# A decode and prefill layer on one core: where passes over cache pages are issued, and which engine takes two products

## The chip, the core and the metric

The kernel runs on one core of a Trainium2 chip. A core has five engines that work side by side, each with its own queue in order: TensorE (PE, matmuls into PSUM), VectorE (DVE), ScalarE (ACT), GpSimd (POOL) and SyncE (SP, which here only issues DMAs). The metric is the device time of one execution in microseconds (us); the median of several runs counts.

## What is computed

One layer of a hybrid decoder, for a prompt of 512 tokens with 16 meta tokens before it, and for eight single new tokens ("sequences"), each with 2048 past positions in a paged cache. An input projection of 2048 columns to 8192 feeds two groups of eight heads, whose gated outputs meet in one output projection:

```python
hq, hk, hv, log_f, hg, aq, ak, av, ag = project(h, norm_g, w_in, lb)   # one matmul, split in eight
S, o = hgrn2_chunked(hq, hk, hv, log_f, s0, chunk)                     # HGRN2 group: a gated linear recurrence
# differential attention group
s = einsum('bqhcd,bkhcd->bchqk', q, k) * 64 ** -0.5 + bias             # c = 0, 1: two softmaxes per head
p = softmax(s, axis=-1)
w = p[:, 0] - lam * p[:, 1]
o_at = einsum('bhqk,bkhv->bqhv', w, v)
h = h + concat(norm(o_hg) * silu(hg), norm(o_at) * silu(ag)) @ w_out   # then a final norm
k_past = cache_k[page_table]                                           # eight sequences x 16 pages of 128 tokens
v_past = cache_v[page_table]
```

For the eight sequences the attention runs over 128 pages of keys and 128 pages of values, 0.5 MB each (128 tokens by 8 heads by 128).

## The kernel before

**The projections set the pace.** The weights are taken in 80 blocks of 128 columns: 64 of the input projection (8 each of aq, ak, av, then hf, hi and hq in turn, then hg, then ag) and 16 of the output projection. A block has four groups of four 128-row pieces. `load_raw` brings weights, `split` (L322) makes a rounded high part on ScalarE (tile hi) and a rest on VectorE (tile lo), three groups ahead (LEAD), and `group` (L337) issues 24 matmuls into the tile ps. The main loop writes one group after another, and between two of them (one "slot") it steps what else is due: `step_threads` runs each waiting generator to its next yield, `value_step` may issue one step of values on TensorE, and `fill` adds VectorE passes over pages. So the order on every engine is fixed when the program is written, and each engine works in that order.

**The kernel's own clock.** While it is written, the program keeps an estimated time for each engine and tile (class `Clock`, L76). Every engine call goes through `Counted` (L141), which estimates its cost and moves that clock; for this reason nearly all instructions have the line L151 in the profile, and tiles tell them apart.

**Prompt attention.** After the block av of a head, `attn` (L910) makes four steps per head, one of 128 queries each, in a pipeline over slots. Scores go to a PSUM tile sc; VectorE adds the bias into the tiles p (two softmaxes) with a row minimum; ScalarE takes the exponential and the sum. Two steps later VectorE makes the reciprocals r, the second one times the factor lambda; ScalarE multiplies the second p by r (L973); then VectorE joins both into p (L976). A step on, TensorE transposes p (tile t_w), and a step after that multiplies values (tile o).

**Keys of the pages.** `page_step` (L675) works on VectorE in two halves per page: page times query (tiles pgt and qb), then a sum over each head's half (tile scd). It may start a sequence s only when the softmax weights of sequence s - 2 are there (flag w) and the values of sequence s - 3 are done (flag pv, KA = 3). Key pages have three buffers (NKB); each finished step issues the next page load on SP's queue. After 16 pages `softmax_dec` makes the weights (tile wd).

**Values of the pages.** For sequences 0 to 5, `value_step` (L702) multiplies two pages by their weights on TensorE: four matmuls of 32 columns side by side (eight records, tile t_pv), and VectorE adds the outcome into acc. Sequences 6 and 7 are named in ONV (L282): for them `dve_value_step` (L733) multiplies a page by the weights head by head on VectorE, eight instructions a page into a tile in the buffer qb, and `pv_sum` (L761) sums over partitions on TensorE at the end. It begins only when the keys of all sequences are done (L741), and each sequence waits for the one before.

**When passes are issued.** `fill` (L603) is called once in a slot and at a few other places. It adds passes as long as VectorE's estimated time is under TensorE's plus LATE (L601), which has a value for each of four stretches: before the block av0, until the last attention head, until the last HGRN head, and after. A key page not landed by then is skipped in favour of a page of values.

**The end of the input projection.** Before the second group of block 63 (L1326), a loop goes on until the norms of all heads and sequences have been written; pages that are left are issued there. The output projection begins after that block.

Of the kernel before, what the change touches and what calls it, by code (L numbers as in the profile page):

```python
# [75 lines left out]
class Clock:  # L76
# [28 lines left out]
                t = b  # L105
        return t

    def issue(self, e, cost, outs, ins, latency=0.08, shared=False):
        start = self.now[e]
        for table, aps in ((self.written, ins + outs), (self.read, outs)):  # L110
            for ap in aps:
                t, by = table.get(ap.tensor.name, (0.0, e))
                if by != e:
                    start = max(start, t + self.LATENCY)
        if e == "pool":
            start = self.port(start)
            self.pool_held = start + cost
        elif shared:
            start = max(start, self.pool_held)
            a, b = self.held[-1]  # L120
            self.held = self.held[-40:]
            if start - b < 0.03:
                self.held[-1] = (a, start + cost)
            else:
                self.held.append((start, start + cost))
        self.now[e] = end = start + cost
        end += latency
        for ap in ins:
            n = ap.tensor.name
            self.read[n] = max(self.read.get(n, (0.0, "")), (end, e))  # L130
        for ap in outs:
            self.written[ap.tensor.name] = end, e
# [6 lines left out]


class Counted:  # L141


    def __init__(self, eng, clock, name):
        self.eng, self.clock, self.name = eng, clock, name

    def __getattr__(self, op):
        f = getattr(self.eng, op)

        def call(*a, **k):  # L150
            r = f(*a, **k)  # L151
            aps = [x for x in a if hasattr(x, "free_size")]
            outs = [x for x in (k.get("out"), k.get("accum_out")) if x is not None]
            if "out" not in k:
                outs.append(aps.pop(0))
            ins = aps + [x for n, x in k.items() if hasattr(x, "free_size") and n not in ("out", "accum_out")]
            n = max(ins[0].free_size(), 1) if op == "tensor_reduce" else (outs[-1] if "out" not in k else outs[0]).free_size()
            late, shared = 0.08, False
            from_psum = any(in_psum(x) for x in ins + outs)
            wide = [x for x in ins if x.free_size() > 1 and not in_psum(x)]  # L160
            if self.name == "pe":
                late = 0.165
                if op == "transpose":
                    t = 0.11
                elif ap_dtype(ins[0]) == F32R:
                    t = max(0.11, n / 2400 + 0.0115)
                else:
                    t = 2 * max(0.118, n / 1200 + min(ins[0].free_size(), P) / 1200)
                    if ins[0].partition_size() == 64:
                        t /= 2  # L170
                    if ins[0].free_size() == 32:
                        t /= 4
            elif self.name == "dve":
                two = op in ("scalar_tensor_tensor", "tensor_tensor_reduce")
                one = op in ("tensor_scalar", "tensor_copy") and not from_psum
                t = (0.13 if two or op == "tensor_scalar" else 0.075) + n / (1920 if one else 960) * (2 if op == "tensor_tensor_scan" else 1)
                if op == "tensor_tensor_reduce":
                    t += 0.13
                shared = len(wide) >= 2 or one and n > 64
            elif self.name == "act":  # L180
                t = n / 1200 + (0.055 if from_psum else 0.095) + (0.09 if hasattr(k.get("scale"), "free_size") or k.get("accum_out") is not None else 0)
            else:
                t = 0.07 + n / 430
            self.clock.issue(self.name, t, outs, ins, late, shared)
            return r
        return call
# [11 lines left out]
def layer_kernel(ctx: ExitStack, tc: tile.TileContext, A):  # L198
# [80 lines left out]

    GK = 4  # L280
    NKB, NPB = 3, 2
    ONV = (6, 7)  # L282
    NG = KC // GK
    LEAD = 3

# [312 lines left out]
                threads.remove(th)  # L598
        return ran

    LATE, SOON = (3.0, 1.5, 4.0, 4.0), 0.0  # L601

    def fill():  # L603

        ph = 0 if "av0" not in flags else 1 if "attn7" not in flags else 2 if "hgrn7" not in flags else 3
        while clock["dve"] < clock["pe"] + LATE[ph]:
            if turn_v[0] and dve_value_step():
                turn_v[0] = 0
                continue
            i = done[0]  # L610
            if i < len(kloaded) and any(clock.written[t.tensor.name][0] > clock["pe"] + SOON for t in (kloaded[i], qbs[ksteps[i][0]])):
                if not dve_value_step():
                    break
                continue
            turn_v[0] = 1
            if not page_step() and not dve_value_step():
                break

    def later(slots, **k):

# [54 lines left out]
    def page_step():  # L675

        i = done[0]
        if i >= len(ksteps):
            return False
        s, g = ksteps[i]  # L680
        z = half[0]
        if z == 0:
            if flags.get("q", slot[0]) >= slot[0] or g == 0 and (s >= 2 and f"w{s - 2}" not in flags or s >= KA and f"pv{s - KA}" not in flags):
                return False
            load_keys(i + 1)
            if g == 0:
                scs[s] = sm.tile([P, NPG + 1, 2 * H], F32, name="scd", bufs=2)
        pt = kloaded[i]
        if z == 0:
            V.tensor_tensor(pt, pt, qbs[s], op=ALU.mult)  # L690
        else:
            V.tensor_reduce(scs[s][:, g, :], pt.rearrange("p (a d) -> p a d", d=64), axis=AX.X, op=ALU.add)
        half[0] = 1 - z
        if z:
            if g == NPG - 1:
                load_q(s + 1)
                spawn(softmax_dec(s), "snew", *([f"w{s - 1}"] if s else []))
            done[0] += 1
            load_keys(i + 1 + NKB)
        return True  # L700
# [32 lines left out]
    def dve_value_step(landed=True):  # L733

        n = vtaken[0]
        s, i = divmod(n, NPG)
        if n >= len(vloaded) or s not in ONV:
            return False
        if flags.get(f"w{s}", slot[0]) >= slot[0] or i == 0 and s and flags.get(f"pv{s - 1}", slot[0]) >= slot[0]:
            return False  # L740
        if i == 0 and done[0] < len(ksteps):  # L741
            return False
        pt = vloaded[n]
        if landed and clock.written[pt.tensor.name][0] > clock["dve"]:
            return False
        if i == 0:
            accs[s] = pg.tile([P, H * P], F32, name="qb", tag="qb")
        for h in range(H):
            cs, w = slice(h * P, (h + 1) * P), ws[s][:, i, h:h + 1]
            if i == 0:  # L750
                V.tensor_scalar(accs[s][:, cs], pt[:, cs], w, None, op0=ALU.mult)
            else:
                V.scalar_tensor_tensor(accs[s][:, cs], pt[:, cs], w, accs[s][:, cs], op0=ALU.mult, op1=ALU.add)
        vtaken[0] += 1
        vdone[0] = vtaken[0] // VB
        load_values()
        if i == NPG - 1:
            spawn(pv_sum(s))
        return True
# [67 lines left out]
    def decode_q():  # L827
        for b in range(2):
            qs = hw.tile([NS, 512], F32, name="qs", tag="t3", bufs=2)
            t = tp("t_q")  # L830
            for h in range(4):
                T.transpose(t[:NS, h * P:(h + 1) * P], aq[:, b * 4 + h, S0:S0 + NS], ident)
            S.activation(qs, t[:NS, :], AF.Copy, scale=-1.0)
            store(out=qd[:, b * 512:(b + 1) * 512], in_=qs)
        load_q(0)
        load_keys(NKB)
        load_values()
        flag("q")
        yield

    def decode_snew():
# [68 lines left out]
    def attn():  # L910
        live = {}
        for n in range(4 * H + 4):
# [53 lines left out]
            if i2:  # L966
                a, jj = i2["head"], i2["j"]
                L1 = (jj + 1) * P + NM
                p0, p1 = i2["p"]
                r = sm.tile([P, 2], F32, name="r")  # L970
                V.reciprocal(r, a["s1"][:, jj, :])
                V.tensor_scalar(r[:, 1:2], r[:, 1:2], nlam, None, op0=ALU.mult)
                S.activation(p1[:, :L1], p1[:, :L1], AF.Copy, scale=r[:, 1:2])  # L973
            fill()
            if i2:
                V.scalar_tensor_tensor(p0[:, :L1], p0[:, :L1], r[:, 0:1], p1[:, :L1], op0=ALU.mult, op1=ALU.add)  # L976
            if n < 4 * H:
                a = head
# [426 lines left out]
```

## Time and profile before

| | |
|---|---|
| median of 3 runs | 1261.57 us (1259.65 to 1262.13) |
| profiled execution | 1256.73 us, of which the span shown is 1254.9 us |
| TensorE busy | 1214.3 us (97%) |
| VectorE busy | 844.9 us (67%) |
| ScalarE busy | 547.8 us (44%) |
| GpSimd busy | 144.7 us (12%) |

A line of a profile names the source line, the engine, the operation, the tile written and the tiles read, and sizes as partitions by elements. Matmuls overlap one another, so a busy TensorE isn't TensorE at its peak. Stretches are given in us from the start of the span: queries and keys are projected until about 250, prompt attention runs until about 460, HGRN until about 900, the gates until 1046, the output projection until the end.

### The profile page before, as it was taken

The numbers are of one execution on the slowest core, as the hardware profiler recorded it, in microseconds if no ns is written. First come the engines' busy times: TensorE is split into PE (matmuls) and PEld (weight loads), VectorE is DVE, ScalarE is ACT, GpSimd is POOL, SyncE is SP. The second block draws the span as 40 slices with busy tenths as digits, with TensorE's granted clock in tenths as the row PEclk, the third lists the DMA queues.
The fourth block names the chain that finished last, engine by engine and source line by source line (L and its number), as shares of the span: only waits on it lengthen the run. The fifth ranks groups of instructions, "written<-read, shape, count | busy, mean of one in ns | idle before, by whom it ended". The sixth has DMA issues, their size and how long they took to land.

```text
span 1254.9 us, 24952 instructions
## 1 busy us (share of the span) xinstructions
PE 1214.3 (97%) x9412; PEld 1096.5 (87%) x9412; DVE 844.9 (67%) x1527; ACT 547.8 (44%) x1288; POOL 144.7 (12%) x151
## 2 busy tenths in 40 slices
PE   8999999999999999999998999999999999999995
PEld 6899999976777779888787888888999999999995
DVE  6522598865666578878668788888997936355253
ACT  6322323355555664545445455554432235223233
POOL 2000001100000001111012010122131410021020
PEclk9999999999999999999999999999999999999998
DMA  7353788935645576889796897987787636433223
GB/s 230 95 161 97 239 275 283 285 103 189 191 163 188 183 234 190 297 272 305 256 318 193 296 307 256 323 286 247 226 287 226 204 101 217 122 89 96 86 68 137
DMA packets 240956, 261.02 MB, mean 208 GB/s; under 512 B 8783, under 2 KB 198962, under 8 KB 240171
## 3 DMA queue, kind: packets, MB, share of 16 engines
q1 hardware_dynamic: 57298, 164.09, 37.5%
q10 hardware_dynamic: 183538, 95.34, 26.9%
q8 instruction: 74, 1.21, 0.4%
q14 instruction: 46, 0.38, 0.1%
HBM read 245.94 MB, written 16.14 MB: 209 GB/s over the span
## 4 chain that ended last, share of the span: by engine, by line
PE 86%; DVE 5%; DMA 4%; ACT 3%; issue 1%; ACTq 1%; SPq 0%; DVEq 0%
PE ps L151 69%; PE t_pv L151 4%; PE o L151 2%; PE ho L151 2%; PE sc L151 1%; DMA raw<-in_w_out 1%; DMA pgt<-in_cache_v 1%; DVE qb L151 1%; PE up L151 1%; PE t_w L151 1%; DVE lo L151 1%; PE at L151 1%; DVE scd L151 1%; PE t_ra L151 1%; PE t_y L151 1%
## 5 line engine op out<-in xcount | busy, mean ns | idle before, releaser
L151 PE MATMUL ps<-xh,hi 128*128 128x264 f32 (+2 forms) x2048 | 539.2, 294 | 3.9 <-ACT gate L151 2.2
L151 PE MATMUL ps<-xl,hi 128*128 128x264 f32 (+2 forms) x2048 | 521.8, 285 | 1.1 <-DVE xl L151 1.1
L151 PEld LDWEIGHTS ps<-xh,hi 128*128 128x128 f32 x2048 | 386.7, 189 | 58.2 <-issue 48.2
L151 PEld LDWEIGHTS ps<-xl,hi 128*128 128x128 f32 x2048 | 386.8, 189 | 2.6 <-issue 2.5
L151 DVE TENSOR_TENSOR lo<-raw,hi 128x512 fp32r<-128x512 f32 x321 | 244.1, 765 | 198.9 <-ACT hi L151 198.3
L151 PE MATMUL ps<-xh,lo 128*128 128x264 f32 (+2 forms) x2048 | 333.8, 285 | 0.0
L151 ACT CAST hi<-raw 128x512 fp32r<-128x512 f32 x321 | 196.3, 617 | 228.7 <-PE ps L151 187.5
L151 PEld LDWEIGHTS ps<-xh,lo 128*128 128x128 f32 x2048 | 284.6, 189 | 0.0
L151 DVE TENSOR_TENSOR pgt<-pgt,qb 128x1024 f32<-128x1024 f32 x128 | 163.7, 1279 | 14.5 <-DMA pgt<-in_cache_k 11.3
L151 DVE TENSOR_REDUCE scd<-pgt 128x16 f32<-128x1024 f32 x128 | 155.0, 1211 | 0.1
L151 PE MATMUL ps<-mh,hi 128*128 128x256 f32 (+1 forms) x512 | 130.0, 286 | 0.5 <-ACT y L151 0.5
L151 PE MATMUL ps<-ml,hi 128*128 128x256 f32 (+1 forms) x512 | 128.5, 283 | 0.0
L151 PEld LDWEIGHTS ps<-mh,hi 128*128 128x128 f32 x512 | 96.4, 188 | 1.0 <-ACT y L151 0.7
L151 PEld LDWEIGHTS ps<-ml,hi 128*128 128x128 f32 x512 | 96.5, 188 | 0.0
L151 PE MATMUL ps<-mh,lo 128*128 128x256 f32 (+1 forms) x512 | 82.5, 283 | 0.0
L151 DVE SCALAR_TENSOR_TENSOR qb<-pgt,wd,qb 128x128 f32<-128x128 f32 x240 | 70.9, 364 | 0.0
L151 PEld LDWEIGHTS ps<-mh,lo 128*128 128x128 f32 x512 | 70.3, 188 | 0.0
L151 PE MATMUL t_pv<-pgt,wd 128*32 128x512 f32 x384 | 53.9, 605 | 12.7 <-ACT wmT L151 4.2
L151 DVE SCALAR_TENSOR_TENSOR p<-p,r,p 128x144 f32<-128x144 f32 (+3 forms) x32 | 18.2, 568 | 71.3 <-ACT p L151 71.2
L151 DVE TENSOR_TENSOR acc<-acc,t_pv 128x512 f32<-128x512 f32 x42 | 28.7, 682 | 23.9 <-PE t_pv L151 23.9
L151 POOL TENSOR_TENSOR sd<-sd,vb 128x1024 f32<-128x1024 f32 x8 | 20.1, 2509 | 183.4 <-ACT vb L151 156.5
L151 ACT COPY hgm<-ho 128x128 f32<-128x128 f32 x32 | 8.5, 265 | 69.5 <-PE ho L151 59.6
(242 smaller groups left out, 1167.2 us busy)
## 6 DMA issues: line engine op xcount, KB each, us to landing
pgt<-in_cache_k SPq DMA_DIRECT2D x128, 512.0 KB
pgt<-in_cache_v SPq DMA_DIRECT2D x128, 512.0 KB
raw<-in_w_in ACTq DMA_DIRECT2D x125, 512.0 KB
raw<-in_w_out ACTq DMA_DIRECT2D x32, 512.0 KB
x<-in_x_prompt SPq DMA_DIRECT2D x4, 1024.0 KB
qb<-qd SPq DMA_DIRECT2D x8, 512.0 KB
sd<-in_state_hgrn SPq DMA_DIRECT2D x8, 512.0 KB
vb<-hvd SPq DMA_DIRECT2D x8, 512.0 KB
```

Of the source, the lines that this page charges most:

```text
L151: r = f(*a, **k)
```

## The change

Three things are changed together.

- **Passes wherever VectorE would wait.** `Counted` gets a hook, `meanwhile`. Before an instruction of VectorE is written, the kernel compares the time at which its inputs are ready by the clock (`ready`, taken out of `issue`) with VectorE's time. As long as the difference is over WAIT = 1.1 us, it writes one more pass: a half of a key page or a page of values (`page`, the choice that `fill` made before). The hook is set when the decode queries are ready. It is off within a pass and within `fill` (`aside`). In the hook a page counts as ready if it has landed 0.3 us after VectorE's time. LATE goes from (3.0, 1.5, 4.0, 4.0) to (2.0, 0.0, 0.5, 3.0).
- **The second softmax's factor.** The multiplication of the second p by r moves from ScalarE to VectorE, right before the instruction that joins both.
- **Three sequences' values on VectorE.** ONV goes from (6, 7) to (5, 6, 7).

```diff
-    def issue(self, e, cost, outs, ins, latency=0.08, shared=False):
-        start = self.now[e]
+    def ready(self, e, outs, ins):
+
+        start = 0.0
         for table, aps in ((self.written, ins + outs), (self.read, outs)):
             for ap in aps:
                 t, by = table.get(ap.tensor.name, (0.0, e))
                 if by != e:
                     start = max(start, t + self.LATENCY)
+        return start
+
+    def issue(self, e, cost, outs, ins, latency=0.08, shared=False):
+        start = max(self.now[e], self.ready(e, outs, ins))
...
 class Counted:
+    WAIT = 1.1
...
+            if self.meanwhile:
+                step, self.meanwhile = self.meanwhile, None
+                while self.clock.ready(self.name, outs, ins) - self.clock[self.name] > self.WAIT and step():
+                    pass
+                self.meanwhile = step
+            r = f(*a, **k)
...
-    ONV = (6, 7)
+    ONV = (5, 6, 7)
...
-    LATE, SOON = (3.0, 1.5, 4.0, 4.0), 0.0
+    LATE, SOON = (2.0, 0.0, 0.5, 3.0), 0.0
+
+    def page(at):
+
+        if turn_v[0] and dve_value_step():
+            turn_v[0] = 0
+            return True
+        i = done[0]
+        if i < len(kloaded) and any(clock.written[t.tensor.name][0] > at for t in (kloaded[i], qbs[ksteps[i][0]])):
+            return dve_value_step()
+        turn_v[0] = 1
+        return page_step() or dve_value_step()
 
     def fill():
 
         ph = 0 if "av0" not in flags else 1 if "attn7" not in flags else 2 if "hgrn7" not in flags else 3
...
+        while clock["dve"] < clock["pe"] + LATE[ph] and aside(lambda: page(clock["pe"] + SOON)):
+            pass
+
+    def aside(step):
+
+        keep, V.meanwhile = V.meanwhile, None
+        r = step()
+        V.meanwhile = keep
+        return r
...
         flag("q")
+        V.meanwhile = lambda: page(clock["dve"] + 0.3)
         yield
...
-                S.activation(p1[:, :L1], p1[:, :L1], AF.Copy, scale=r[:, 1:2])
             fill()
             if i2:
+                V.tensor_scalar(p1[:, :L1], p1[:, :L1], r[:, 1:2], None, op0=ALU.mult)
                 V.scalar_tensor_tensor(p0[:, :L1], p0[:, :L1], r[:, 0:1], p1[:, :L1], op0=ALU.mult, op1=ALU.add)
```

## Rows read from the trace of the kernel before

**Rows 1.** The page: span, busy time of each engine, chain that ended last.
```profile
span 1254.9 us, 24952 instructions
PE 1214.3 (97%) x9412; PEld 1096.5 (87%) x9412; DVE 844.9 (67%) x1527; ACT 547.8 (44%) x1288; POOL 144.7 (12%) x151
...
PE 86%; DVE 5%; DMA 4%; ACT 3%; issue 1%; ACTq 1%; SPq 0%; DVEq 0%
```
**Rows 2.** Waits of TensorE: who waited for whom, us total, times, longest.
```profile
PE t_pv L151 <- ACT wmT L151: 4.2, 6, 0.7
...
PE t_pv L151 <- DVE wd L151: 3.7, 1, 3.7
PE t_pv L151 <- DVE st L151: 2.6, 3, 1.0
PE ps L151 <- ACT gate L151: 2.2, 3, 0.9
...
PE t_pv L151 <- DVE scd L151: 0.6, 1, 0.6
```
**Rows 3.** Busy time by stretches: length, each engine (instructions), TensorE's clock, DMA.
```profile
300.00:325.00 25.00, 23.95 (x161) 18.40 (x160) 15.87 (x45) 13.59 (x42) 0.71 (x4) 1.00 0.52 174
...
675.00:700.00 25.00, 21.33 (x156) 18.65 (x155) 19.20 (x25) 9.48 (x26) 5.21 (x4) 0.93 0.77 244
...
900.00:925.00 25.00, 24.12 (x198) 23.71 (x198) 24.92 (x80) 8.10 (x16) 7.13 (x5) 1.00 0.91 295
...
1025.00:1050.00 25.00, 25.00 (x210) 25.00 (x209) 15.84 (x33) 14.13 (x28) 2.35 (x3) 1.00 0.30 86
```
**Rows 4.** TensorE in order of time: start, duration, instruction, idle time before it.
```profile
287.02 1.06 PE L151 MATMUL t_pv<-pgt,wd 128*32 128x512 f32 x8 [0.71 <-ACT wmT L151]
288.01 0.39 PE L151 MATMUL ps<-xh,hi 128*128 128x272 f32 x1
...
952.17 1.05 PE L151 MATMUL t_pv<-qb,ones 128*32 128x512 f32 x4
953.15 0.39 PE L151 MATMUL ps<-xh,hi 128*128 128x256 f32 x1
```
**Rows 5.** Groups of VectorE by shape: count, busy us, mean ns, idle before.
```profile
L151 DVE SCALAR_TENSOR_TENSOR qb<-pgt,wd,qb 128x128 f32<-128x128 f32 x240 | 70.9, 364 | 0.0
L151 DVE TENSOR_TENSOR acc<-acc,t_pv 128x512 f32<-128x512 f32 x42 | 28.7, 682 | 23.9 <-PE t_pv L151 23.9
...
L151 DVE TENSOR_SCALAR qb<-pgt,wd 128x128 f32<-128x128 f32 x16 | 4.4, 350 | 0.0
...
L151 DVE TENSOR_SCALAR xr<-xr,rfin 128x512 f32<-128x512 f32 x6 | 2.6, 483 | 1.3 <-ACT rfin L151 1.3
```
**Rows 6.** The tile pgt: ns min/median/max, first and last start us, shapes.
```profile
L151 DVE SCALAR_TENSOR_TENSOR qb<-pgt,wd,qb x240: 329/340/1386, 902.7 to 1004.5; 128x128 f32<-128x128 f32 x120
...
L151 DVE TENSOR_TENSOR pgt<-pgt,qb x128: 1203/1216/2522, 139.6 to 896.5; 128x1024 f32<-128x1024 f32 x128
L151 DVE TENSOR_REDUCE scd<-pgt x128: 1187/1211/1220, 141.3 to 898.8; 128x16 f32<-128x1024 f32 x128
```
**Rows 7.** Groups of ScalarE by shape, the factor on the second p.
```profile
L151 ACT ACTIVATE p<-p,r 128x528 f32<-128x528 f32 x8 | 5.8, 720 | 0.0
...
L151 ACT ACTIVATE p<-p,r 128x144 f32<-128x144 f32 x8 | 3.2, 400 | 0.0
```
**Rows 8.** Waits of VectorE: us total, times, longest.
```profile
DVE p L151 <- ACT p L151: 71.2, 30, 5.5
```
**Rows 9.** VectorE's busy time with the tile scd, by stretches.
```profile
225.00:250.00 25.00, 8.79 (x10) 1.00 0.90 284
...
400.00:425.00 25.00, 2.42 (x2) 1.00 0.59 191
```
**Rows 10.** The tile mh: matmuls of the output projection, first and last start.
```profile
L151 PE MATMUL ps<-mh,hi x512: 274/283/391, 1045.9 to 1240.3; 128*128 128x256 f32 x86, 128*128 128x264 f32 x85
```
**Rows 11.** VectorE in order of time: the last norm of the sequences' attention.
```profile
1018.89 0.28 DVE L151 SCALAR_TENSOR_TENSOR oSa<-oSa,gat,sqs 128x64 f32<-128x64 f32 x1
```

More of the change, by code (lines that the diff above doesn't have):

```diff
@@ L141 @@
 class Counted:
+    WAIT = 1.1
     def __init__(self, eng, clock, name):
         self.eng, self.clock, self.name = eng, clock, name
+        self.meanwhile = None
     def __getattr__(self, op):
@@ L150, in call @@
         def call(*a, **k):
-            r = f(*a, **k)
             aps = [x for x in a if hasattr(x, "free_size")]
@@ L599, in step_threads @@
         return ran
-    LATE, SOON = (3.0, 1.5, 4.0, 4.0), 0.0
+    LATE, SOON = (2.0, 0.0, 0.5, 3.0), 0.0
[8 more added lines that the diff above has]
+        return page_step() or dve_value_step()
     def fill():
         ph = 0 if "av0" not in flags else 1 if "attn7" not in flags else 2 if "hgrn7" not in flags else 3
[L606 to L617, printed above, removed]
+        while clock["dve"] < clock["pe"] + LATE[ph] and aside(lambda: page(clock["pe"] + SOON)):
[5 more added lines that the diff above has]
+        return r
     def later(slots, **k):
```

## The prediction

> **What bounds the kernel now.** I read the page's busy shares first, then the chain of work that ended last, then the waits of TensorE, and only then the other engines. The reader is to see in the first two that TensorE is the bound: it is busy 97% of the span, and 86% of the chain runs through it [rows 1]. The waits of TensorE say how little of this is waiting: the longest kinds are 4.2, 3.7, 2.6 and 2.2 us [rows 2]. So a cut in VectorE's or ScalarE's work is worth nothing by itself; what counts is work taken from TensorE, and the few us for which it stands still. VectorE has room, but unevenly: 15.9 us of 25 busy in the attention stretch, 19.2 in the HGRN stretch, 24.9 in the stretch that multiplies values [rows 3]. The last is where a VectorE bound could come from.
>
> **Part 1, sequence 5's values go from TensorE to VectorE (ONV).** On TensorE a value step is eight matmul records; one starts at 287.02 and the next projection matmul at 288.01, so it holds the array for 0.99 us [rows 4]. A sequence has eight steps: 7.9 us leave. The new sum over partitions (pv_sum) comes in once; its like ran from 952.17 to 953.15, 0.98 us [rows 4]. The transposes at the end are as many as before. Net: 6.9 us less on TensorE, which is on the path. I count no further wait with it, since a wait before a value step may pass to whatever stands there next; if it goes too, that belongs to the larger gain below.
> On VectorE, seven additions of 0.68 us and one copy, bounded by the same row, go: 5.5 us. In come 8 products at 0.350 and 120 at 0.364 us [rows 5]: 46.5 us, so 41 us more. They cost nothing as long as they end before TensorE needs them; that cover is worked out under the rivals, as it is the weak point.
> Here two rows speak for caution: one product of this kind took 1386 ns against a median of 340, and one page multiply 2522 against 1216 [rows 6]. If one product in each of the 48 pages were held as the longest was, 48 x 1.05 = 50 us would be added to VectorE; by the mean of the row, which has in it what this trace had of such holds, nothing is. I take the mean and carry the 50 us into the last rival. The Trainium skill, page "SBUF — State Buffer", section "Who interferes with whom", gives holds a cause: a VectorE instruction with two SBUF inputs and a GpSimd instruction that reads SBUF exclude each other for a whole instruction. By that rule the end would be the slower rival's; by the row's mean it is the forecast's.
>
> **Part 2, the second softmax's factor goes from ScalarE to VectorE.** ScalarE loses 32 activations, 5.8 us for the eight widest and 3.2 for the eight narrowest, so about 18 us in all over four widths [rows 7]. VectorE gains 32 one-source multiplies by a column. The nearest rows are 350 ns at 128 elements and 483 at 512 [rows 5]; the widths here are 144 to 528, so 11 to 16 us; I take 13.5. What goes is VectorE's wait for that activation: 71.2 us in 30 waits [rows 8]. Nothing of it is on TensorE's path today: its waits show none for the weights p. Late next is the product of scores on TensorE (the tile sc), which VectorE takes right after, so the 71 us become another idle time on VectorE unless passes over pages fill them. Worth to the end time: zero. If the cover failed (VectorE too late with p), the transposes t_w would wait up to 0.48 us per step, 32 x 0.48 = 15 us at the very worst.
>
> **Part 3, passes are issued where VectorE would wait (meanwhile, page, ready).** No arithmetic is added. The written order changes: before any VectorE instruction whose inputs the kernel's own clock puts more than 1.1 us away, a key pass or a page of values is put in. What is queued behind it starts up to one pass late, 1.21 us for a key pass [rows 6], 2.9 for a page of eight products [rows 5]. Each key step also issues its page load on SP's queue earlier, ahead of loads of strip, sd and vb that it now passes; the loads are the same in number. The reader of a later instruction is TensorE or ScalarE; TensorE has no wait for lo among its waits, so I count zero for the split of weights, and bound the rest by the third rival.
> The use is that pages get done earlier. In 225:250 VectorE spent 8.8 us on sums of pages, in 400:425 only 2.4, two pages [rows 9]; idle time in the attention stretch is 9.1 us of 25, 73 us from 250 to 450, less part 2's 13.5: room for 59 / 2.43 = 24 pages, a page being 1.22 + 1.21 us. Keys of sequence 3 have to wait for the values of sequence 0 (page_step), so I take 12 to 24.
>
> **Part 4, LATE falls from (3, 1.5, 4, 4) to (2, 0, 0.5, 3).** fill() lets VectorE's planned time run that many us past TensorE's before it stops adding passes. In the HGRN stretch it was 4, and there TensorE waits for late VectorE work: 3.7 for the weights wd, 2.6 for st, 0.6 for scd [rows 2], 6.9 us. Behind the 3.7 the granted clock was 0.93 in 675:700 [rows 3], so some 3.5 us ran at 1.2 GHz and cost half, 1.75 us. Together 8.65 us that stem from lateness. With 0.5 in place of 4 a pass may still stand ahead (1.2), so lateness goes from about 5.2 to 1.7 us of plan. All of it may go (-8.65), none, or, since denser passes make new lateness, as much may come (+8.65). I take -4.3: the one wait of 3.7 is cut to the 1.7 that the plan still allows, 2.0, and the slow clock behind it with it, 1.75; of the other 3.2 us, in waits of 1.0 at most, I count 0.55.
>
> **Sum.** -6.9 - 4.3 = -11.2 us. The profiled execution took 1256.7 us (span 1254.9), the median of the runs is 1261.6, 4.8 more; on the profile's base 1245.5, on the median's 1250.4. I give the latter: 1250.5 us.
>
> **Rivals.**
> *The larger gain.* All lateness goes, and with ScalarE freed also its share: 6.9 + 8.65 + 4.2 (value steps waiting for wmT) + 2.2 (ps for gate) = 22 us, 1239.6. For it: every one of these waits has an engine behind it that gets lighter or earlier. Against: wmT is copied after the transposes on TensorE whatever ScalarE did before, and 2.2 arises where VectorE is full.
> *VectorE fuller and later, the gain given back.* The kernel's clock puts a product at 0.26 us where the row has 0.34, so the plan sees waits that the chip doesn't have, and passes stand in front of work that is due. Sixteen waits like the six of 0.7 us for wmT would eat the 11.2 us: 1261.6. For it: 80 passes and more are moved; against: TensorE's waits for VectorE are few today although LATE let VectorE lag 4 us.
> *Slower: the values end too late.* Sequence 5's values may start only when all keys are done (dve_value_step), and block 63's second group stands behind the values of all sequences. TensorE reaches it three groups, 72 matmuls at 25/210 us [rows 3], before 1045.9 [rows 10]: 1037.3, and 11 less after the change, 1026. From the last product (1004.5) to the normalized sums (1018.9) went 14.4 us [rows 6, 11], so the last product must start by 1012. Thirty pages took 1004.5 - 902.7 = 101.8 us, 3.4 each [rows 6]; 48 take 163. So keys must end by 849; today they end at 898.8 [rows 6]. Each us later than 849 is a us on the path; with no page done earlier it is 50, 1300. For it: 24.9 of 25 busy there already. Against: 128 key pages went at 757.5 / 127 = 6.0 us each, so 12 pages moved into idle time bring the end to 827, 24 to 756, where 849 would do; and the HGRN stretch has 5.8 idle of 25 more. It decides if fewer than nine pages are moved, or if held products cost their 50 us. Likely size: 10 to 25 us past the limit, 1261 to 1276.
>
> **How the numbers follow.** My forecast, 1245 to 1256, has 0.54; the larger gain, 1239 to 1245, 0.13; given back, within 0.2%, 0.14; slower 0.19, of which 0.03 is held products. 0.2% is 2.5 us, about what a measurement of this kernel can tell from no change. Faster is then 0.67, same 0.14, slower 0.19. The range 1239 to 1264 takes in the first three and leaves out most of the last: 0.81.
>
> **What would show it.** TensorE's records of t_pv over pages fall from 384 to 320, and its busy time by about 7 us. VectorE's wait for the activation on p is gone, its idle in 250:450 is well under 9 us of 25, and the last key sum starts near 760 to 830. The waits of t_pv for wd, st and scd are under 3.5 us together, and no stretch has a clock below 1.0. Wrong would be: products that run on past 1012, TensorE waiting near block 63, or new waits for lo, nm, p or st of more than 5 us in sum. The sum would also be wrong if the value steps of sequences 0 to 4 came to wait for pages, behind key loads on SP's queue.

## The result

The change takes 1245.4 us (median of four runs, 1243.1 to 1246.5) against 1261.9 us before: 16.5 us less, a ratio of 0.9867 with a 95% interval of 0.9846 to 0.9889. The prediction was 1250.5 us, 1239 to 1264.

The page of the changed kernel, with the lines that answer to [rows 1]:

```profile
span 1243.3 us, 24937 instructions
...
PE 1207.9 (97%) x9352; PEld 1094.5 (88%) x9352; DVE 897.7 (72%) x1678; ACT 532.6 (43%) x1255; POOL 143.2 (12%) x151
...
PE 79%; DVE 10%; DMA 4%; ACT 3%; issue 2%; ACTq 1%; SPq 0%; DVEq 0%
```

TensorE is still the bound, with 6.4 us less of busy time and 60 records fewer. VectorE has 53 us more work, ScalarE 15 us less. VectorE's share of the chain has gone from 5% to 10%. The waits of TensorE, as [rows 2]:

```profile
PE t_pv L168 <- ACT wmT L168: 4.6, 6, 0.9
...
PE t_pv L168 <- DVE st L168: 2.4, 3, 1.2
...
PE ho L168 <- DVE am L168: 0.8, 1, 0.8
...
PE ps L168 <- ACT gate L168: 0.4, 1, 0.4
```

The wait of 3.7 us for wd is gone, and those for st, scd and wd together went from 6.9 to 2.4 us; the waits for wmT stayed. The stretches, as [rows 3], in the columns length, engines, clock and DMA:

```profile
300.00:325.00 25.00, 23.92 (x161) 17.55 (x159) 21.31 (x50) 12.11 (x38) 1.02 (x4) 1.00 0.66 211
325.00:350.00 25.00, 23.95 (x158) 18.83 (x155) 21.20 (x53) 10.56 (x31) 0.83 (x5) 0.93 0.63 213
...
675.00:700.00 25.00, 25.00 (x201) 21.71 (x201) 21.52 (x25) 14.58 (x35) 4.79 (x4) 1.00 0.88 296
...
900.00:925.00 25.00, 25.00 (x204) 23.81 (x203) 18.19 (x59) 6.88 (x13) 7.18 (x4) 1.00 0.72 206
```

VectorE is busy 21.3 us of 25 in the attention stretch, where it was 15.9. The clock of 675:700 is back at 1.00, but 325:350 and three other stretches of attention show 0.93. In the first trace of the kernel before it was 1.00 throughout attention, for instance here:

```profile
325.00:350.00 25.00, 23.95 (x167) 18.47 (x167) 16.67 (x50) 13.34 (x37) 0.77 (x5) 1.00 0.60 191
```

Last the pages, as [rows 6], [rows 10] and [rows 11]:

```profile
L168 DVE SCALAR_TENSOR_TENSOR qb<-pgt,wd,qb x360: 332/345/2482, 845.8 to 1006.5; 128x128 f32<-128x128 f32 x180
L168 DVE TENSOR_REDUCE scd<-pgt x128: 1193/1215/1223, 140.2 to 839.9; 128x16 f32<-128x1024 f32 x128
...
L168 PE MATMUL ps<-mh,hi x512: 274/283/390, 1034.4 to 1228.3; 128*128 128x256 f32 x86, 128*128 128x264 f32 x85
...
1021.86 0.28 DVE L168 SCALAR_TENSOR_TENSOR oSa<-oSa,gat,sqs 128x64 f32<-128x64 f32 x1
```

Keys end at 839.9 instead of 898.8, the products of three sequences run from 845.8 to 1006.5, and the output projection starts 11.5 us earlier. The profiled executions differ by 11.6 us only (1256.7 and 1245.1), the medians by 16.5; the second trace of the kernel before, below, shows where most of the other 5 us are in one execution.

### The profile page after: what moved, and what is told of

It reads as the page before. It is cut to its first block, busy times and chain, and to the rows that moved or that the text cites. A ratio compares the mean times of both kernels' runs of the same rounds, so it can differ in the third digit from the quotient of the medians.

```text
span 1243.3 us, 24937 instructions
## 1 busy us (share of the span) xinstructions
PE 1207.9 (97%) x9352; PEld 1094.5 (88%) x9352; DVE 897.7 (72%) x1678; ACT 532.6 (43%) x1255; POOL 143.2 (12%) x151
## 4 chain that ended last, share of the span: by engine, by line
PE 79%; DVE 10%; DMA 4%; ACT 3%; issue 2%; ACTq 1%; SPq 0%; DVEq 0%
PE ps L168 65%; PE t_pv L168 4%; DVE qb L168 2%; DVE pgt L168 2%; DVE scd L168 2%; PE o L168 1%; PE ho L168 1%; DVE lo L168 1%; DMA raw<-in_w_out 1%; PE sc L168 1%; DMA raw<-in_w_in 1%; PE up L168 1%; PE t_w L168 1%; PE at L168 1%; DVE p L168 1%
## 5 line engine op out<-in xcount | busy, mean ns | idle before, releaser
L168 DVE TENSOR_TENSOR lo<-raw,hi 128x512 fp32r<-128x512 f32 x321 | 253.5, 795 | 216.5 <-ACT hi L168 215.6
L168 DVE TENSOR_TENSOR pgt<-pgt,qb 128x1024 f32<-128x1024 f32 x128 | 156.3, 1221 | 11.7 <-DMA pgt<-in_cache_k 7.0
L168 DVE SCALAR_TENSOR_TENSOR qb<-pgt,wd,qb 128x128 f32<-128x128 f32 x360 | 106.8, 371 | 0.0
L168 PE MATMUL t_pv<-pgt,wd 128*32 128x512 f32 x320 | 48.2, 648 | 8.5 <-ACT wmT L168 4.6
L168 ACT ACTIVATE p<-p,nm 128x144 f32<-128x144 f32 (+3 forms) x64 | 36.1, 565 | 2.0 <-DVE nm L168 2.0
L168 DVE TENSOR_TENSOR xr<-xr,t_y 128x512 f32<-128x512 f32 (+1 forms) x17 | 11.2, 657 | 31.2 <-PE t_y L168 31.2
```

## The experiments

Times are medians of the timed runs; ratios are to the kernel before on the same chip. "Alone" means one part put into the kernel before; "without" means the change less one part. Every variant also writes its own order of instructions, but for the one that keeps the order of before.

| kernel | us | ratio, 95% interval |
|---|---|---|
| change | 1245.4 | 0.9867 (0.9846 to 0.9889) |
| third sequence alone | 1272.6 | 1.0077 (1.0060 to 1.0093) |
| factor alone | 1251.5 | 0.9916 (0.9900 to 0.9933) |
| LATE alone | 1397.4 | 1.1067 (1.1048 to 1.1085) |
| passes and LATE alone | 1259.8 | 0.9978 (0.9961 to 0.9995) |
| change without the factor | 1248.5 | 0.9904 (0.9874 to 0.9935) |
| change without the third sequence | 1254.4 | 0.9940 (0.9914 to 0.9965) |
| factor and third sequence, no passes | 1254.7 | 0.9944 (0.9927 to 0.9961) |
| change with the old LATE | 1251.8 | 0.9932 (0.9909 to 0.9955) |
| factor alone in the order of before | 1258.8 | 0.9967 (0.9949 to 0.9985) |
| LATE one us longer in attention | 1265.3 | 1.0044 (1.0026 to 1.0061) |
| change, no value step beside se | 1241.0 | 0.9852 (0.9836 to 0.9869) |

### Third sequence alone

```diff
-    ONV = (6, 7)
+    ONV = (5, 6, 7)
```

> The kernel before with sequence 5's values on VectorE and nothing else of the change. My theory: TensorE loses about 7 us of work, but no page is done earlier, so the keys end near 899 as before, 48 pages of products at 3.4 us end near 1060, and TensorE waits for them before the second group of block 63: 1275 to 1305 us. Rival (the end of the values isn't near the path, the array's work is all that counts): 1250 to 1257 us.

Measured 1272.6 us, 10.2 more than before. The direction and the place are those of my theory, the size is less. The tile pgt, then TensorE at block 63's second group:

```profile
L151 DVE SCALAR_TENSOR_TENSOR qb<-pgt,wd,qb x360: 330/340/1390, 897.1 to 1047.2; 128x128 f32<-128x128 f32 x180
...
L151 DVE TENSOR_REDUCE scd<-pgt x128: 1196/1212/1220, 141.7 to 893.3; 128x16 f32<-128x1024 f32 x128
```
```profile
1046.65 2.87 PE L151 MATMUL t_pv<-qb,ones 128*32 128x512 f32 x4 [14.85 <-DVE qb L151]
```

With keys at 893.3 the products end past 1047, and TensorE stands still for 14.85 us. The matmuls behind it take 2.87 us where their like took 1.05 [rows 4]: the granted clock fell to half within the wait and stayed there until 1049.9. So the slower rival is real; what keeps the change out of it is that its keys end 53 us earlier than here.

### Factor alone

```diff
-                S.activation(p1[:, :L1], p1[:, :L1], AF.Copy, scale=r[:, 1:2])
             fill()
             if i2:
+                V.tensor_scalar(p1[:, :L1], p1[:, :L1], r[:, 1:2], None, op0=ALU.mult)
```

> The kernel before with the second softmax's factor on VectorE and nothing else. My theory: TensorE waits for none of it, so 1259 to 1265 us, VectorE's wait of 71 us for the activation on p gone and most of it found again as waits for the scores. Rival (ScalarE's 18 us stood in the way of the copies of wT and wmT that TensorE waits for): 6 us faster or more, 1256 or less.

Measured 1251.5 us, 10.9 less. I had given this part nothing, and this is the largest gain of any part alone. It isn't the rival's either: the waits of t_pv for wmT are as long as before (4.6 us). And of VectorE's 71.2 us only 29.4 came back as waits for scores (17.5 for the tile se, 11.9 for sc), not most of it. Two traces stand beside each other here, first the kernel before, run a second time, then the factor alone:

```profile
PE t_pv L151 <- DMA pgt<-in_cache_v: 4.8, 4, 3.1
...
PE t_pv L151 <- DVE wd L151: 3.7, 1, 3.7
...
PE ps L151 <- ACT gate L151: 2.0, 3, 0.8
PE t_pv L151 <- DVE st L151: 1.6, 2, 1.0
```
```profile
PE ps L151 <- ACT gate L151: 3.1, 1, 3.1
...
PE t_pv L151 <- DMA pgt<-in_cache_v: 1.4, 1, 1.4
...
PE t_pv L151 <- DVE scd L151: 0.5, 1, 0.5
```

Counting records of ps, group by group, the factor alone reaches block 32 some 2 us later (562.5 against 560.6), but with three value steps more behind it, so it is about 1 us ahead in work; it reaches block 50 10 us earlier (867.9 against 878.1), with as many value steps done. So most of the gain arises in the HGRN stretch, where no factor is computed at all: the waits for wd and for pages fall there. That isn't TensorE waiting for the factor in its own place, and two experiments below (the factor alone in the order of before, and LATE one us longer) were made to settle it.

### The kernel before, once more

> The kernel before once more, for a second trace: the first one is of an execution of 1256.7 us, and its timed runs lie at 1257 to 1264. Expected at 1260 to 1264 us; the difference should be found either in stretches at 1.2 GHz (1.7 us each) or in longer waits of t_pv for VectorE's late work.

1261.1 us, with the same program as the first trace (1256.7). One wait differs:

```profile
600.30 1.05 PE L151 MATMUL t_pv<-pgt,wd 128*32 128x512 f32 x4 [3.05 <-DMA pgt<-in_cache_v]
601.68 1.05 PE L151 MATMUL t_pv<-pgt,wd 128*32 128x512 f32 x4 [0.33 <-DMA pgt<-in_cache_v]
```

In the first trace no wait of TensorE for a page was over 0.8 us. The written order lets a value step stand at a point where its page may or may not have landed. Besides that there are two stretches of 3.4 us at half clock ahead of the output's end instead of one, and other waits are shorter: in all TensorE waits 2.4 us more and is busy 2.0 us more. The first trace was of an execution at the quick end, and a sum of terms made against it was small against the median.

### LATE alone, and passes with LATE alone

```diff
-    LATE, SOON = (3.0, 1.5, 4.0, 4.0), 0.0
+    LATE, SOON = (2.0, 0.0, 0.5, 3.0), 0.0
```

> The kernel before with LATE at (2, 0, 0.5, 3) and nothing else: fewer passes may be issued ahead of other VectorE work. My theory: the waits of t_pv for wd, st and scd fall from 6.9 us to under 3.5, but without passes in the waits the keys end later than 899 and the values of sequences 6 and 7 come near the limit of about 1020; so 1255 to 1275 us. Rival (LATE alone carries the gain): 1245 to 1253 us.

Measured 1397.4 us, far outside what I expected. Three stretches of it, then its longest waits of TensorE:

```profile
300.00:325.00 25.00, 23.95 (x161) 17.48 (x160) 12.16 (x39) 14.18 (x43) 0.71 (x4) 1.00 0.42 138
...
600.00:625.00 25.00, 24.87 (x201) 21.70 (x200) 12.46 (x15) 15.11 (x33) 4.77 (x4) 1.00 0.62 210
...
1100.00:1125.00 25.00, 1.59 (x5) 1.09 (x5) 24.36 (x93) 0.43 (x1) 0.00 (x0) 0.50 0.80 271
```
```profile
PE t_pv L151 <- DVE qb L151: 51.3, 2, 32.4
PE t_mx L151 <- DVE mx L151: 38.8, 2, 34.6
```

With nothing else to issue passes, VectorE is busy 12 us of 25, and pages are left over at block 63, where TensorE then has 1.6 us of work in 25. It had reached that block at 1016.7, 17.6 us earlier than before (1034.3). Half of that is work not yet done: TensorE was busy 8.8 us less by then, five value steps among it. The other half, 8.8 us, is waits that are gone. So less lateness did help the array; but from there to the end it takes 158 us more than before, for the pages left over.

The passes put in the waits make up for this. The part is `meanwhile` with the new LATE, factor on ScalarE, ONV (6, 7):

```diff
+        V.meanwhile = lambda: page(clock["dve"] + 0.3)
```

> The change without its other two parts: passes issued where VectorE would wait, LATE at the new values, factor on ScalarE, values of sequences 6 and 7 alone on VectorE. My theory: the late work of VectorE is earlier, 4 to 9 us of TensorE's waits go and 7 us of value steps stay: 1252 to 1258 us; keys end near 840. Rival (the passes are the whole gain, the moved values are nothing): 1243 to 1248 us.

Measured 1259.8 us, 2.6 less and above the range that I expected; the keys end at 819. So the passes aren't the whole gain, against the rival, and almost none by themselves. TensorE's waits fell to 24.3 us, from 27.5 and 29.9 in the two traces of before, but two new ones of 5.4 us are among them, with 13.7 us of half clock around them (see the change without the factor). What the passes do for the third sequence is seen by leaving them out:

### Factor and third sequence, without passes

Both diffs above in the kernel before, with its LATE.

> The factor and the third sequence, without the passes in the waits and with LATE as before. My theory: keys end near 887 as with the factor alone, so the products end past the limit and TensorE waits 10 to 20 us before block 63's second group: 1255 to 1266 us; the passes are what makes the third sequence pay. Rival, that the passes are not needed: 1243 to 1248 us.

Measured 1254.7 us: by ratio 3.5 us more than the factor alone, with an uncertainty of some 3. That is just under what I expected, in time and in waits, and far from the rival. The last key sum starts at 873.9, the last product at 1031.4, and TensorE waits:

```profile
PE t_pv L151 <- DVE qb L151: 9.0, 1, 9.0
```

### The change without the third sequence

```diff
-    ONV = (5, 6, 7)
+    ONV = (6, 7)
```

> The change with the values of sequences 6 and 7 alone on VectorE. My theory: TensorE keeps 8 value steps of 0.99 us, so 7 us slower than the change, 1251 to 1254 us. Rival, that the steps only fill time in which TensorE would wait: 1244 to 1248 us.

Measured 1254.4 us. The ratios 0.9940 and 0.9867 lie 0.0073 apart, 9.2 us, with an uncertainty of some 4; 7 were expected. With passes and new LATE in place the moved values are worth their work on the array; whether more, the runs don't tell.

### The change without the factor

```diff
+                S.activation(p1[:, :L1], p1[:, :L1], AF.Copy, scale=r[:, 1:2])
             fill()
             if i2:
-                V.tensor_scalar(p1[:, :L1], p1[:, :L1], r[:, 1:2], None, op0=ALU.mult)
```

> The change with the factor left on ScalarE. If parts add up (the factor alone gave 10.9 us, the passes with LATE 2.6), it is 1252 to 1257 us. Rival, that factor and passes cure the same waits of TensorE for VectorE, so that the factor adds nothing once the passes are there: 1243 to 1248 us.

Measured 1248.5 us, by ratio 0.0037 from the change, 4.7 us, and the two intervals overlap. It lies between both expectations. The trace has what I had missed. VectorE, then TensorE at about the same time:

```profile
420.27 0.50 DVE L168 SCALAR_TENSOR_TENSOR p<-p,r,p 128x272 f32<-128x272 f32 x1 [2.86 <-ACT p L168]
...
421.58 0.17 DVE L168 CUSTOM_DVE_ANT_0 p<-se,strip 128x16 f32<-128x16 f32 x1
```
```profile
417.43 0.41 PE L168 MATMUL se<-kt,aq 128*128 128x32 f32 x2
418.64 0.39 PE L168 MATMUL t_mb<-ident,m 16*128 16x16 f32 x2 [0.80 <-ACT wmT L168]
421.86 1.93 PE L168 MATMUL t_pv<-pgt,wd 128*32 128x512 f32 x8 [2.83 <-issue]
```

VectorE waits 2.86 us for the factor at the head of its queue. Behind it stand the two instructions that read the scores in the PSUM tile se. Such tiles take turns in two buffers: t_mb has the one and se the other, so t_pv, which is next, needs se's. The value step starts at 421.86, 0.11 us after the second read of se has ended (421.75); it is 2.83 us late and runs at half clock (1.93 us). The profile names no releaser here, so the link to the buffer is read from the order of the records.

There are two such waits, 5.6 us in all. The second, 2.81 us, ends 0.11 us after a read of se too, but there VectorE waited only 0.59 us for the factor, and a key pass (2.5 us) stood ahead; what it shares with the first is that a tile of the pages' softmax (t_sum) stands between se and t_pv. The trace of passes and LATE alone has the same two waits at the same places. In the change no such tile stands there, and neither wait occurs. So one wait for the factor did come to lie on TensorE's path; but half of the 5.6 us, at least, hangs on the order in which the tiles are written.

### The factor alone, in the order of before

The kernel's clock goes on counting the activation on ScalarE, so that every engine has its instructions of before in their order, but for the factor:

```diff
-                S.activation(p1[:, :L1], p1[:, :L1], AF.Copy, scale=r[:, 1:2])
+                clock.issue("act", L1 / 1200 + 0.185, [p1[:, :L1]], [p1[:, :L1], r[:, 1:2]])
             fill()
             if i2:
+                nc.vector.tensor_scalar(p1[:, :L1], p1[:, :L1], r[:, 1:2], None, op0=ALU.mult)
```

> The factor on VectorE with the written order of the kernel before: the kernel's clock still counts the activation on ScalarE, so every engine has the instructions of before in their order, but for the factor itself. If the 10.9 us of the factor alone come from VectorE's wait that is gone, they come here too: 1249 to 1254 us. If they come from the other order that the kernel's clock then writes (another choice of where passes and value steps stand), nothing is left: 1258 to 1264 us.

Measured 1258.8 us, 0.9967 of before: 4.2 us less. In the two traces TensorE, VectorE, ScalarE and GpSimd have the same instructions in the same order, but for the factor. So it is neither: some 4 of the factor's 10.6 us (by ratio, with an uncertainty of 2) come from the edit, and some 6 (with one of 3) from the other order that the kernel's clock writes once it knows of the edit. Where the 4 us lie isn't shown: the trace is of an execution of 1260.7 us. The wait of 3.7 us for wd is there, unchanged:

```profile
PE t_pv L151 <- DVE wd L151: 3.7, 1, 3.7
```

### LATE one us longer in attention

```diff
-    LATE, SOON = (3.0, 1.5, 4.0, 4.0), 0.0
+    LATE, SOON = (3.0, 2.5, 4.0, 4.0), 0.0
```

> The kernel before with LATE at (3, 2.5, 4, 4): only in the attention stretch may passes run one us further, so keys come somewhat earlier and later instructions fall in another order; the factor stays on ScalarE. If the factor's 10.9 us came from such a shift (the wait of 3.7 us for wd and those for page loads fall elsewhere), this gives a good part of it too: 1250 to 1257 us. If they came from the factor's own wait on VectorE, it stays at 1259 to 1264 us.

Measured 1265.3 us, slower by 0.0044. The keys end earlier (872 against 899). Under the waits of TensorE the one for wd is no longer named; the longest are these:

```profile
PE t_pv L151 <- issue: 6.4, 2, 3.5
...
PE t_sum L151 <- DVE rs L151: 2.6, 1, 2.6
```

The longer of the two without a releaser is, by its timing, the wait for wd all the same, in another place. VectorE, then TensorE:

```profile
647.59 0.29 DVE L151 TENSOR_TENSOR wd<-scd 128x128 f32<-128x128 f32 x1
```
```profile
647.99 1.11 PE L151 MATMUL t_pv<-pgt,wd 128*32 128x512 f32 x8 [3.50 <-issue]
```

The value step starts 0.11 us after wd is written. The other one, 2.9 us, is for se again, with t_mx ahead of t_pv. Earlier keys by another small shift of the order thus cost 5 us where the factor's shift gave 6. Whether the factor's better order follows from anything but chance stays open.

### The change with the old LATE

```diff
-    LATE, SOON = (2.0, 0.0, 0.5, 3.0), 0.0
+    LATE, SOON = (3.0, 1.5, 4.0, 4.0), 0.0
```

> The change with LATE left at (3, 1.5, 4, 4). My prediction's theory, that lateness of VectorE's work is set by LATE: waits of t_pv and others for st, scd, wd and am grow from 3.2 to about 7 us and the time to 1249 to 1254 us. Rival, that LATE does nothing of its own once passes stand in the waits: 1243 to 1248 us.

Measured 1251.8 us, 0.0065 or 8.2 us behind the change, with an uncertainty of some 4. LATE does carry that much, in the range I had given for lateness. But the waits that grow are others than I had named:

```profile
PE t_pv L168 <- ACT wmT L168: 5.0, 6, 1.1
PE t_pv L168 <- DMA pgt<-in_cache_v: 4.4, 5, 1.4
...
PE ho L168 <- DVE am L168: 2.9, 1, 2.9
...
PE t_pv L168 <- DVE st L168: 2.0, 2, 1.0
```

Those for st are no longer than in the change (2.4), scd and wd don't appear, am has grown by 2.1 us, and waits for value pages are the longest new kind. The keys end at 796 here, 44 us before the change's, since more passes are issued early; the value steps on TensorE then wait for their pages.

The table has one more comparison. This run is the factor and the third sequence with the old LATE, and with the passes; without them it was 0.9944, with them it is 0.9932, no difference that the runs show. The passes do end the keys 78 us earlier, and the wait of 9.0 us for qb is gone; yet the time shows little of it until LATE is lowered with them: 0.9867.

### The change, no value step beside se

In the last step of each head the tile se takes one of the two PSUM buffers that t_pv needs. There, a value step is left to the next slot:

```diff
                     e_ = tp("se")
+                    full[0] = slot[0]
...
-        if n >= len(vsteps):
+        if n >= len(vsteps) or full[0] == slot[0]:
             return
```

> The change, but no value step on TensorE in a slot whose attention step has the tile se, where t_pv waits 0.7 to 0.9 us for the copy of wmT, once per head, and where in the change's profile all four stretches at 1.2 GHz begin. Theory that these waits are worth themselves and what the slow clock behind them costs: 4.4 us of waits and up to 6.6 us of clock go, 1235 to 1241 us. Rival, that the wait passes to the next user of the PSUM buffers, or that values done a slot later make keys and products late: 1244 to 1250 us.

Measured 1241.0 us (1240.7 to 1242.1): 0.9852 of before, where the change has 0.9867; the intervals overlap, so that it beats the kernel before is shown, and that it beats the change isn't. The six waits of t_pv for wmT, 4.6 us, and all slow clock in the attention stretch are gone (one wait of 0.7 us for wmT is left, before t_mx). What came in their place:

```profile
PE ho L168 <- DVE am L168: 3.5, 1, 3.5
PE t_pv L168 <- DMA pgt<-in_cache_v: 2.1, 2, 1.2
...
PE t_pv L168 <- ACT wT L168: 2.0, 2, 1.5
PE t_mx L168 <- DVE mx L168: 1.6, 1, 1.6
```

The waits of TensorE, 21.6 us in all in both traces, have moved. The slow clock cost less: one stretch of 6.8 us, behind the wait for am, where the change has four of 3.4, so some 3.4 us lost instead of 6.8.

## Why the prediction was right, and where its terms were not

- **The bound and the place of the gain: right, the agreement in part luck.** TensorE's busy time fell by 6.4 us, "about 7" was the sign I had named, and the records of t_pv over pages fell by 64. But in the 6.4 us are some 5 that the change loses by more half clock (four stretches of 3.4 us against one), so without them it would have fallen by some 11; that estimate goes by half of their length, and what else left the busy time isn't traced. The measured gain is 16.5 us by the medians where the sum had 11.2. On the base of the profiled executions it is 11.6; the remaining 5 are for the most part the slower typical run of before, as in the second trace with its page wait of 3.05 us. Against the second trace of before TensorE waits 8.3 us less and is busy 8.4 us less. The range was wide, and the parts left out of the change one by one make 9.2, 8.2 and 4.7 us, 22 in sum, so that the total came out near the sum of two terms says less for the terms than the runs on each do. My list of TensorE's longest waits had left one out, 4.0 us for the tile x; it lies in the first part of the kernel and changes no term.
- **Third sequence: right in kind, small.** Forecast -6.9; with passes and new LATE present it is worth 9.2, with an uncertainty of some 4 us.
- **Its cover: right, by luck in one number.** I had the limit for keys at 849, 163 us for 48 pages and TensorE at block 63's second group at 1026. Keys ended at 839.9, the products took 162.8 us from the first page's first (843.7), and TensorE came there at 1025.7 without a wait. The 163 were misread: in the 101.8 us of thirty pages lay the first page of sequence 7 too, which is another instruction in [rows 5], so they were 31 pages at 3.3 us, 158 us for 48; the change's pages took longer, 3.4. The guess of 756 to 827 for the keys was too early by 13 us. The last norm ended at 1022.1, so the margin was 3.6 us, not the 22 of that guess. Held products didn't decide: one took 2482 ns, but the mean was 371 after 364. The rival's mechanism is shown by the third sequence alone (14.85 us of wait) and with the factor (9.0).
- **Lateness (LATE): right in sign and range, wrong in its waits.** Forecast -4.3 within +-8.65; measured 8.2 in place, with an uncertainty of some 4. The waits for wd, st and scd fell as I said, under 3.5 us. But "no stretch has a clock below 1.0" was wrong: the change's trace has four stretches of half clock in attention, 6.8 us in all by half of their length, more than in the kernel before. So part of the term was given back, and part of what LATE earns lies in waits for pages and for am that I didn't price.
- **The factor: the step that failed.** "Worth to the end time: zero" was wrong. Its costs were right: VectorE's 12.6 us for 13.5 forecast, and the wait of 71.2 us for p gone, with 5.7 and 4.0 us found again as waits for scores. Alone it gave 10.6 us by ratio, 4.2 with the order kept, and 4.7, not clear of zero, on top of the rest. Two things were missing. An edit in a kernel that writes its order by an estimated clock changes the order everywhere, and I had priced the edit only. And a wait at the head of an in-order queue holds up what stands behind it for other engines (2.86 us of VectorE's, 2.83 us of TensorE's); I had looked only at who reads p.
- **The passes: right, zero by themselves.** 2.6 us alone with LATE, and on top of the factor no gain that the runs show (0.9940 after 0.9916). Together with the lower LATE they carry the third sequence: without both it cost some 3 us on top of the factor, with both it gave 9. With the old LATE the passes added no gain that the runs show (0.9932 after 0.9944).

The parts alone sum to +10.2 - 10.9 - 2.6 = -3.3 us; together they gave -16.5. The gain is in the combination: the passes make room on VectorE before the deadline, and the third sequence spends it. The factor makes none there: alone it ended the keys 12 us earlier (887 against 899), but with the passes they end at 814 without it and at 840 with it. Since each variant also has its own order, and order alone moved the time by 5 or 6 us in two cases (the factor's other order, and LATE one us longer in attention), what a single part is worth stays uncertain by about as much.

## What to carry to other kernels

Where the array is the bound, moving work off it pays only as long as the engine that takes it has room before a known deadline: work out when that engine must be done, and which part of a change makes the room. In a kernel that plans its order by an estimate, price the new order, not only the edit, and keep the order fixed in one experiment to tell them apart. Before summing terms against one trace, see where its time lies among the runs: here it was 5 us below the median.

## What was not expected of the hardware

The waits of t_pv for wmT are as short as 0.7 to 0.9 us, and there are six in each of these traces. In the first trace of the kernel before none was followed by a slow clock, in the second one, in the change's four. Their length doesn't decide: in the change a wait of 0.71 us was followed by it, another of 0.74 us was not. One of the change's four, the value step and the matmuls behind it, then the window that has it:

```profile
284.56 1.94 PE L168 MATMUL t_pv<-pgt,wd 128*32 128x512 f32 x8 [0.78 <-ACT wmT L168]
286.43 0.60 PE L168 MATMUL ps<-xh,hi 128*128 128x272 f32 x1
286.82 0.43 PE L168 MATMUL ps<-xl,hi 128*128 128x272 f32 x1
```
```profile
275.00:300.00 25.00, 23.64 (x149) 16.67 (x146) 22.21 (x55) 10.39 (x31) 0.06 (x1) 0.93 0.71 231
```

The value step takes 1.94 us for the 1.06 of [rows 4], and the matmuls 0.43 for some 0.29: the array runs at 1.2 GHz for 3.4 us. So a wait of 0.78 us here cost some 1.7 us more than itself, and a like one elsewhere nothing more. In the change with no value step beside se, which has none of these waits before a value step, there is no slow clock in the attention stretch at all. Why one such wait is followed by it and the next isn't stays open.
